# Memory's norm split around a merge, and low parts of weights moved to GpSimd

## The chip, the cores and the metric

The kernel runs on one core of one Trainium2 chip. The metric is device time in microseconds (us). The kernel before was run three times: 906.31, 908.57 and 908.62 us, median 908.57 us. The profile is of one more execution, which took 907.74 us.

## The reference, cut to what matters

The reference is one block of a network on 512 tokens of width 1024: a mixer of three attention branches, then attention to a memory of 256 rows, then a feed-forward part, each added to the stream, and a last norm. The change touches where the mixer's branches are merged and where memory's keys and values are made:

```python
merged = (g[:, :, 0] * (o_a @ w_up[0]) + g[:, :, 1] * (o_b @ w_up[1]) + g[:, :, 2] * (o_c @ w_up[2]))
h = h + merged @ w_out
kv = (_rmsnorm(mem, norm_mem_kv) @ w_mem_kv)      # 256 rows, 512 columns: keys and values
def _rmsnorm(x, g):
    return x * rsqrt(mean(x * x) + 1e-6) * g
```

Branch b is the one whose keys are selected by a top-k; its merge comes last.

## The kernel before, in words

All is float32. A weight or an activation goes to TensorE as two parts that the engine takes at a higher rate: a high part (`whi`, a rounding cast, L60) and a low part (`wlo`, the difference, L68). A product is three matmuls (`mm3`, L96 to L98): high by high, high by low, low by high. ScalarE (ACT) does the casts, VectorE (DVE) most of the differences, GpSimd (POOL) those of the weights that come through the ring `load_fill`. The other ring, `load_split`, has three buffers of 128x1024 each for the raw weights, the high parts and the low parts; a load of raw weights (SyncE's queue, SP) starts when the difference that read that buffer three loads before is done.

A list scheduler sets the order of the instructions on each engine when the kernel is built. Each engine then takes its list strictly in order, and an instruction waits on semaphores for what it needs.

The places that matter, in the order of the program:

- `fill_gate(1, f, S // 2)`: gates of branch b for the first 256 tokens; eight products into the PSUM tile `gf`, and TensorE's last work before memory's norm.
- Memory's norm. The 256 rows of `mem` are two chunks, `h[0]` and `h[1]`. For each, `norm_t` squares the chunk and sums it (ACT L129), turns the sum into a scale in eight VectorE instructions of 128x1 elements (`rms_scale`, L117 to L122, tile `rs`), multiplies (DVE L131, into `h[2]` or `h[3]`), transposes the result in eight 128x128 blocks (PE L135, tile `ps`), and splits it from PSUM into the two parts `mem_t`, which are the second halves of `mg_hi` and `mg_lo`.
- kv: 48 matmuls of 512 columns with four loads of `w_mem_kv` into two PSUM banks (tile `gm`), then copies, and transposes of the keys (L676 to L681).
- `merge_up(1, "b", ...)` for the first 256 tokens: for each of eight blocks f, six matmuls of 256 columns with `w_up` into a `gm` bank (two banks in turn), then on VectorE the sum with the gate (L388, reads PSUM and frees the bank) and an add (L401, both inputs in SBUF), then the split into `mg_hi` (ACT) and `mg_lo` (GpSimd).
- `w_out` for these tokens: 96 matmuls of 512 columns with eight loads of `w_out` (tile `wo`), then memory's attention for them (`memory_pair`). The other 256 tokens follow in the same way (`merge_rest`, `w_out`, `memory_pair`), then the feed-forward part.

Of the kernel before, what the change touches and what calls it, by code (L numbers as in the profile page):

```python
# [16 lines left out]
S = 512  # L17
D = 1024
# [8 lines left out]
def block_kernel(ctx: ExitStack, tc: tile.TileContext, A, out, dbg=None):  # L27
    nc = tc.nc
    w_in = A["w_in"][0]

    def pool(stack, name, side="left", **kw):
        return stack.enter_context(tc.tile_pool(name=name, bufs=1, side=side, reuse_waits="tile", **kw))
# [25 lines left out]
    def copy(eng, dst, src):  # L58
        if eng is nc.scalar:
            nc.scalar.copy(dst, src)  # L60
        else:
            eng.tensor_copy(dst, src)

    def split(dst_hi, dst_lo, src, hi_eng=None, lo_eng=None, scale=None):

        if scale is None:
            copy(hi_eng or nc.scalar, dst_hi, src)
            (lo_eng or nc.vector).tensor_sub(dst_lo, src, dst_hi.bitcast(F32))  # L68
        else:
            nc.scalar.activation(dst_hi, src, AF.Copy, scale=scale)  # L70
            nc.vector.scalar_tensor_tensor(dst_lo, src, scale, dst_hi.bitcast(F32), op0=ALU.mult, op1=ALU.subtract)

    def ring(pl, bufs, hi_eng=None, lo_eng=None):

        def load(shape, parts, lo_eng=lo_eng):
            n = shape[0] * shape[1]
            raw = pl.tile([P, WT], F32, name="raw", bufs=bufs[0])
            rv = raw[:, :n].rearrange("p (k n) -> p k n", n=shape[1])
            off = 0
            for src in parts:  # L80
                w = src.shape[-1]
                nc.sync.dma_start(rv[:, :, off:off + w], src)
                off += w
            hi = pl.tile([P, WT], F32R, name="whi", bufs=bufs[1])
            lo = pl.tile([P, WT], F32R, name="wlo", bufs=bufs[1])
            split(hi[:, :n], lo[:, :n], raw[:, :n], hi_eng, lo_eng)
            return [t[:, :n].rearrange("p (k n) -> p k n", n=shape[1]) for t in (hi, lo)]
        return load

    load_split = ring(stage, (3, 3))  # L90
# [14 lines left out]
    def col_view(w, c0, n):  # L105
        return w.rearrange("(k p) n -> p k n", p=P)[:, :, c0:c0 + n]

    def rms_scale(wk, ss, logs=False):

        v = wk.tile([P, 3], F32, name="rs", bufs=3)  # L110
        w, y, t = (v[:, i:i + 1] for i in range(3))
        if logs:
            nc.vector.tensor_scalar(w, ss, -0.5 / D, -0.5e-6, op0=ALU.mult, op1=ALU.add)
            nc.scalar.activation(y, ss, AF.Ln, bias=eps, scale=1.0 / D)
            nc.scalar.activation(y, y, AF.Exp, scale=-0.5)
        else:
            nc.vector.tensor_scalar(w, ss, 0.5 / D, 0.5e-6, op0=ALU.mult, op1=ALU.add)  # L117

            nc.vector.tensor_scalar(y.bitcast(I32), w.bitcast(I32), -0.5, 1597463007.0 - 2.0 ** 22 - 2.0 ** 31, op0=ALU.mult, op1=ALU.add)
        for _ in range(1 if logs else 3):  # L120
            nc.vector.scalar_tensor_tensor(t, y, w, y, op0=ALU.mult, op1=ALU.mult)
            nc.vector.scalar_tensor_tensor(y, t, 1.5 if logs else -1.5, y, op0=ALU.add, op1=ALU.mult)  # L122
        return y

    def norm_t(wk, ps, src, gain, dst, cols, logs=False, u=None):
        ss = wk.tile([P, 1], F32, name="ss", bufs=2)
        if u is None:
            u = wk.tile([P, D], F32, name="u", bufs=NT if logs else 2)
        nc.scalar.activation(u, src, AF.Square, accum_out=ss)  # L129
        y = rms_scale(wk, ss, logs)  # L130
        nc.vector.scalar_tensor_tensor(u, src, y, gain, op0=ALU.mult, op1=ALU.mult)  # L131
        for b in range(2):
            tp = ps.tile([P, 4, P], F32, name="ps")
            for k in range(4):
                nc.tensor.transpose(tp[:, k, :], u[:, (4 * b + k) * P:(4 * b + k + 1) * P], ident)  # L135
            split(dst[0][:, 4 * b:4 * b + 4, cols], dst[1][:, 4 * b:4 * b + 4, cols], tp)

    def load_gain(wk, name, bufs=1):
        g = A[name]
        g = g[0] if len(g.shape) == 2 else g  # L140
        t = wk.tile([P, D], F32, name="gain", bufs=bufs)
        nc.scalar.dma_start(t, g.partition_broadcast(P))
        return t
# [4 lines left out]
    def cc(c):  # L148
        return slice(c * P, (c + 1) * P)
# [7 lines left out]
    ps = p1.enter_context(tc.tile_pool(name="ps1", bufs=5, space=PSUM))  # L157
    gm_ps = gf_ps
# [29 lines left out]
    wk = pool(wk_st, "wk", side="right")  # L188
# [3 lines left out]
    gain = wk.tile([P, D], F32, name="gain")  # L192
# [7 lines left out]
    for c in range(NT):  # L200
        norm_t(wk, ps, xts[c], gain, uT, cc(c), logs=True)
# [178 lines left out]
    def load_up(j, fh, load):  # L380
        return load((2, 512), [A["w_up"][0, j].rearrange("(k p) n -> p k n", p=P)[:, :, fh * 512:(fh + 1) * 512]])

    def add_up(w, f, name, g, up, cols):

        fc = slice(f % 4 * P, f % 4 * P + P)
        for k in range(2):
            mm3(up, [t[:, k, fc] for t in w], [t[:, k, cols] for t in oT[name]], k == 0, k == 1)
        nc.vector.scalar_tensor_tensor(g, g, 1.0, up, op0=ALU.add, op1=ALU.mult)  # L388

    def merge_up(j, name, load, up_ps, n=S):  # L390
        for f in range(NK):
            if f % 4 == 0:
                w = load_up(j, f // 4, load)
            g, first = g_t[j, f][:, :n], g_t[0, f][:, :n]
            if j == 0 and f < early_g:
                with tc.issue_after(last_exp[0]):
                    nc.scalar.activation(g, g, AF.Tanh, scale=0.5)
            up = up_ps.tile([P, 512], F32, name=up_tag[up_ps is gf_ps])
            add_up(w, f, name, g, up[:, :n], slice(0, n))
            if j == 1:  # L400
                nc.vector.tensor_add(first, first, g)  # L401
                split(mg[0][:, f, :n], mg[1][:, f, :n], first, lo_eng=nc.gpsimd)
            elif j == 2:
                nc.gpsimd.tensor_add(first, first, g)
# [7 lines left out]
    ps = pm.enter_context(tc.tile_pool(name="ps2", bufs=3, space=PSUM))  # L412
    gm_ps = pm.enter_context(tc.tile_pool(name="gm_ps", bufs=2, space=PSUM))
# [237 lines left out]
    h = [hp_.tile([P, D], F32, name=f"h{c}") for c in range(NT)]  # L651
# [7 lines left out]
    mem_t = [t[:, :, half1] for t in mg]  # L659
    kv_st = ctx.enter_context(ExitStack())  # L660
    kvp = pool(kv_st, "kvp")
    for c in range(2):
        nc.scalar.dma_start(h[c], A["mem"][0, cc(c), :])
    gain = load_gain(kvp, "norm_mem_kv")
    for c in range(2):
        norm_t(kvp, ps, h[c], gain, mem_t, cc(c), u=h[2 + c])
    kv_acc = [gm_ps.tile([P, 512], F32, name="gm") for c in range(2)]
    for k2 in range(0, NK, 2):
        wh, wl = load_split((2, 512), [col_view(A["w_mem_kv"][0], 0, 512)[:, k2:k2 + 2, :]])
        for kk in range(2):  # L670
            for c in range(2):
                k = k2 + kk
                mm3(kv_acc[c], [t[:, k, cc(c)] for t in mem_t], (wh[:, kk, :], wl[:, kk, :]), k == 0, k == NK - 1)
# [7 lines left out]
        nc.vector.tensor_copy(vm[:, c, :], kvt[:, 256:512])  # L681
    kv_st.close()

    merge_up(1, "b", load_split, gm_ps, S // 2)
    first1 = [h[2 + f // 4][:, f % 4 * 256:f % 4 * 256 + 256] for f in range(NK)]
    for f in range(NK):
        nc.scalar.copy(first1[f], g_t[0, f][:, half1])
# [7 lines left out]
    ps = d_st.enter_context(tc.tile_pool(name="pd_ps", bufs=2, space=PSUM))  # L695
# [21 lines left out]
    def memory_pair(cs):  # L717
        pr = {}
        for c in cs:
            norm_t(md, ps, h[c], gain_q, uT, cc(c))  # L720
# [55 lines left out]
    for cp in range(2):  # L776
        cs = (2 * cp, 2 * cp + 1)
        if cp:
            merge_rest(0)
            merge_rest(1)  # L780
        for c in cs:
            nc.scalar.dma_start(h[c], A["x"][0, cc(c), :])
        ob = {(c, half): wo_ps.tile([P, 512], F32, name="wo") for c in cs for half in range(2)}
        for k in range(NK):
            w = load_split((1, D), [col_view(A["w_out"][0], 0, D)[:, k:k + 1, :]])
            for c in cs:
                for half in range(2):
                    n = slice(half * 512, half * 512 + 512)
                    mm3(ob[c, half], [t[:, k, cc(c)] for t in mg], [t[:, 0, n] for t in w], k == 0, k == NK - 1)
        for c in cs:  # L790
            for half in range(2):
                n = slice(half * 512, half * 512 + 512)
                nc.vector.tensor_add(h[c][:, n], ob[c, half], h[c][:, n])
        memory_pair(cs)
# [52 lines left out]
    y_out, gain = (utp.tile([P, NK, S], F32, name=n).rearrange("p a b -> p (a b)") for n in ("ut_hi", "ut_lo"))  # L847
    gain = gain[:, 0:D]
# [76 lines left out]
```

## Time and profile before

| | |
|---|---|
| median of 3 runs | 908.57 us (906.31 to 908.62) |
| profiled execution | 907.74 us, of which the span is 905.9 us |
| TensorE busy | 861.6 us, 95% of the span |
| VectorE, ScalarE, GpSimd busy | 508.0, 411.9, 139.6 us |
| mean granted TensorE clock | 0.989 of full |
| memory's norm to the end of the first `w_out` | about 377 to 428 us of the span |

The profile's timelines have one row for an instruction, or for several of one kind merged (xN): start, duration, engine, source line, operation, output and inputs; in brackets how long the engine sat idle before it and what ended that. An instruction's duration includes the time in which it was issued but held up. A table by stretches has, for each, from and to, its length, the busy time of PE, PEld, DVE, ACT and POOL (with the instructions), TensorE's granted clock as a part of full, the share of the DMA engines and GB/s. The chain of waits is followed back from the last instruction; its rows are start, length and what took it.

### The profile page before, as it was taken

Reading aid. Unit: us, or ns where it says so; the run is one execution under the profiler, and the core shown is the slowest. Engines: PE = TensorE matmul, PEld = TensorE weight load, DVE = VectorE, ACT = ScalarE, POOL = GpSimd, SP = SyncE. Lnnn points to the kernel's source line nnn. Section 1 sums busy time; section 2 is a strip of 40 time slices with the busy share of each in tenths; the row PEclk is TensorE's granted clock in tenths of the full one; section 3 lists DMA queues with packets and bytes.
Section 4 is the critical chain, followed back from the end, with each engine's and each line's share of the span. In section 5 each row is a group of like instructions: output and inputs, shape, how many; then the busy total and the mean of one; then the engine's idle time right before and its main releaser. Section 6 shows DMA issues by size and latency. Waiting matters only on the chain.

```text
span 905.9 us, 13081 instructions
## 1 busy us (share of the span) xinstructions
PE 861.6 (95%) x5012; PEld 734.7 (81%) x5012; DVE 508.0 (56%) x1155; ACT 411.9 (45%) x779; POOL 139.6 (15%) x116
## 2 busy tenths in 40 slices
PE   5999999899999999799989999999999999999995
PEld 5987899787677877787878879998888888888884
DVE  4466377689993058666677758653344443322226
ACT  6388545558872235454655555432322322211123
POOL 4021232201213472221232020000000000000002
PEclk9999999899999999999999999999999999999998
DMA  9240114410103331557455523553332333322312
GB/s 322 81 109 24 52 49 130 127 48 24 48 24 98 96 103 53 163 181 247 131 155 177 180 71 114 182 163 101 93 94 93 95 105 103 116 93 93 96 45 93
DMA packets 93710, 99.00 MB, mean 109 GB/s; under 512 B 4656, under 2 KB 81616, under 8 KB 93648
## 3 DMA queue, kind: packets, MB, share of 16 engines
q1 hardware_dynamic: 91568, 92.75, 33.7%
q10 hardware_dynamic: 2080, 5.42, 1.8%
q8 instruction: 39, 0.64, 0.3%
q14 instruction: 23, 0.19, 0.1%
HBM read 96.06 MB, written 2.10 MB: 108 GB/s over the span
## 4 chain that ended last, share of the span: by engine, by line
PE 82%; DVE 9%; ACT 3%; DMA 2%; issue 2%; POOL 0%; ACTq 0%; SPq 0%; DVEq 0%; POOLq 0%
PE wo L97 9%; PE wo L98 9%; PE wo L96 9%; PE gf L98 5%; PE gf L97 5%; PE gf L96 5%; PE ff L98 4%; PE ff L97 4%; PE ff L96 4%; PE gm L96 3%; PE gm L97 3%; PE gm L98 2%; PE av L103 2%; PE y L98 2%; PE y L97 2%; PE y L96 2%
## 5 line engine op out<-in xcount | busy, mean ns | idle before, releaser
L60 ACT CAST whi<-raw 128x1024 fp32r<-128x1024 f32 (+1 forms) x167 | 174.6, 1048 | 289.3 <-PE y L98 78.9
L68 DVE TENSOR_TENSOR wlo<-raw,whi 128x1024 fp32r<-128x1024 f32 (+1 forms) x131 | 164.4, 1257 | 207.4 <-ACT whi L60 207.2
L68 POOL TENSOR_TENSOR wlo<-raw,whi 128x1024 fp32r<-128x1024 f32 x36 | 87.9, 2446 | 329.7 <-ACT whi L60 279.3
L97 PE MATMUL wo<-ut_lo,whi 128*128 128x256 f32 (+1 forms) x320 | 106.1, 332 | 0.0
L98 PE MATMUL wo<-ut_hi,wlo 128*128 128x256 f32 (+1 forms) x320 | 105.2, 329 | 0.0
L96 PE MATMUL wo<-ut_hi,whi 128*128 128x256 f32 (+1 forms) x320 | 105.0, 328 | 0.0
L96 PE MATMUL gf<-ut_hi,whi 128*128 128x512 f32 (+1 forms) x192 | 69.9, 364 | 0.0
L97 PE MATMUL gf<-ut_lo,whi 128*128 128x512 f32 (+1 forms) x192 | 69.8, 364 | 0.0
L98 PE MATMUL gf<-ut_hi,wlo 128*128 128x512 f32 (+1 forms) x192 | 69.8, 363 | 0.0
L98 PE MATMUL ff<-ut_hi,wlo 128*128 128x512 f32 (+1 forms) x192 | 68.0, 354 | 0.0
L97 PE MATMUL ff<-ut_lo,whi 128*128 128x512 f32 (+1 forms) x192 | 68.0, 354 | 0.0
L96 PE MATMUL ff<-ut_hi,whi 128*128 128x512 f32 (+1 forms) x192 | 68.0, 354 | 0.0
L97 PEld LDWEIGHTS wo<-ut_lo,whi 128*128 128x128 f32 x320 | 61.6, 193 | 6.3 <-issue 1.0
L96 PEld LDWEIGHTS wo<-ut_hi,whi 128*128 128x128 f32 x320 | 61.5, 192 | 5.7 <-issue 0.7
L98 PEld LDWEIGHTS wo<-ut_hi,wlo 128*128 128x128 f32 x320 | 61.5, 192 | 5.5 <-issue 0.4
L874 POOL TENSOR_TENSOR ut_hi<-ut_hi,ut_lo 128x512 f32<-128x512 f32 x4 | 5.0, 1271 | 367.0 <-ACT ut_hi L873 367.0
L96 PE MATMUL gm<-whi,ut_hi 128*128 128x256 f32 (+1 forms) x160 | 47.7, 298 | 0.0
L97 PE MATMUL gm<-wlo,ut_hi 128*128 128x256 f32 (+1 forms) x160 | 47.2, 295 | 0.0
L98 PE MATMUL gm<-whi,ut_lo 128*128 128x256 f32 (+1 forms) x160 | 46.5, 291 | 0.0
L98 PEld LDWEIGHTS gf<-ut_hi,wlo 128*128 128x128 f32 x192 | 36.3, 189 | 6.7 <-issue 1.9
L96 PEld LDWEIGHTS gf<-ut_hi,whi 128*128 128x128 f32 x192 | 36.3, 189 | 6.0 <-issue 1.2
L97 PEld LDWEIGHTS gf<-ut_lo,whi 128*128 128x128 f32 x192 | 36.3, 189 | 5.3 <-issue 0.8
(329 smaller groups left out, 2032.0 us busy)
## 6 DMA issues: line engine op xcount, KB each, us to landing
raw<-in_w_ffn_in_dram SPq DMA_DIRECT2D x56, 512.0 KB, 3.6
raw<-in_w_in_dram SPq DMA_DIRECT2D x46, 512.0 KB, 3.9
raw<-in_w_ffn_out_dram SPq DMA_DIRECT2D x22, 512.0 KB, 3.6
raw<-in_w_out_dram SPq DMA_DIRECT2D x16, 512.0 KB, 3.6
raw<-in_w_up_dram SPq DMA_DIRECT2D x8, 512.0 KB, 4.3
xt<-in_x_dram SPq DMA_DIRECT2D x4, 512.0 KB, 9.1
raw<-in_w_mem_kv_dram SPq DMA_DIRECT2D x4, 512.0 KB, 3.7
raw<-in_w_mem_q_dram SPq DMA_DIRECT2D x4, 512.0 KB, 3.9
```

Of the source, the lines that this page charges most:

```text
L60: nc.scalar.copy(dst, src)
L68: (lo_eng or nc.vector).tensor_sub(dst_lo, src, dst_hi.bitcast(F32))
L96: nc.tensor.matmul(dst, lh, rh, start=first, stop=False, skip_group_check=True)
L97: nc.tensor.matmul(dst, lh, rl, start=False, stop=False, skip_group_check=True)
L98: return nc.tensor.matmul(dst, ll, rh, start=False, stop=last, skip_group_check=True).ins
L103: nc.tensor.matmul(dst[64 * x:64 * x + 64], lhs[x], rhs[x], start=first, stop=last, skip_group_check=True)
L874: nc.gpsimd.tensor_mul(yo[:, n], yo[:, n], gain[:, n])
```

## The change: what it does

`norm_t` is split into `norm_rows` (squares, scale, multiplication) and `turn` (transposes and the split into two parts). For memory, both chunks' `norm_rows` now stand first, then `merge_up(1, "b", ...)`, then both chunks' `turn`, then kv. So branch b's merge moves from behind kv to between the two parts of the norm. Three sets of weights' low parts change engine: the two of `w_up` in this merge go from VectorE to GpSimd, two of the four of `w_mem_kv`, and four of the eight of `w_out`, each of the two times that it is used. That is 12 instructions of 128x1024 elements more on GpSimd and 12 fewer on VectorE.

```diff
-    def norm_t(wk, ps, src, gain, dst, cols, logs=False, u=None):
+    def norm_rows(wk, src, gain, logs=False, u=None):
...
         nc.scalar.activation(u, src, AF.Square, accum_out=ss)
         y = rms_scale(wk, ss, logs)
         nc.vector.scalar_tensor_tensor(u, src, y, gain, op0=ALU.mult, op1=ALU.mult)
+        return u
+
+    def turn(ps, u, dst, cols):
         for b in range(2):
...
+    def norm_t(wk, ps, src, gain, dst, cols, logs=False):
+        turn(ps, norm_rows(wk, src, gain, logs), dst, cols)
...
     for c in range(2):
-        norm_t(kvp, ps, h[c], gain, mem_t, cc(c), u=h[2 + c])
+        norm_rows(kvp, h[c], gain, u=h[2 + c])
+    merge_up(1, "b", lambda *a: load_split(*a, lo_eng=nc.gpsimd), gm_ps, S // 2)
+    for c in range(2):
+        turn(ps, h[2 + c], mem_t, cc(c))
     kv_acc = [gm_ps.tile([P, 512], F32, name="gm") for c in range(2)]
     for k2 in range(0, NK, 2):
-        wh, wl = load_split((2, 512), [col_view(A["w_mem_kv"][0], 0, 512)[:, k2:k2 + 2, :]])
+        wh, wl = load_split((2, 512), [col_view(A["w_mem_kv"][0], 0, 512)[:, k2:k2 + 2, :]],
+                            (nc.vector, nc.gpsimd)[k2 // 2 % 2])
...
-    merge_up(1, "b", load_split, gm_ps, S // 2)
...
-            w = load_split((1, D), [col_view(A["w_out"][0], 0, D)[:, k:k + 1, :]])
+            w = load_split((1, D), [col_view(A["w_out"][0], 0, D)[:, k:k + 1, :]], (nc.vector, nc.gpsimd)[k % 2])
```

GpSimd's list at memory's norm, before. `wlo_4914` and `wlo_4944` are the low parts of `w_mem_q`, `mg_lo` those of the merged rows, `wlo_5071` is `w_mem_o`:

```order
L68 TENSOR_TENSOR wlo_4914<-raw_4911,whi_4913 128x1024
L68 TENSOR_TENSOR wlo_4944<-raw_4941,whi_4943 128x1024
L68 TENSOR_TENSOR mg_lo_4425<-g_1119,mg_hi_4424 128x256
L68 TENSOR_TENSOR mg_lo_4425<-g_1152,mg_hi_4424 128x256
L68 TENSOR_TENSOR mg_lo_4425<-g_1185,mg_hi_4424 128x256
```

The same place now. `wlo_4460` and `wlo_4510` are `w_up`, `wlo_4608` is the second load of `w_mem_kv`:

```order
L68 TENSOR_TENSOR wlo_4460<-raw_4457,whi_4459 128x1024
L68 TENSOR_TENSOR wlo_4510<-raw_4507,whi_4509 128x1024
L68 TENSOR_TENSOR wlo_4914<-raw_4911,whi_4913 128x1024
L68 TENSOR_TENSOR wlo_4944<-raw_4941,whi_4943 128x1024
L68 TENSOR_TENSOR mg_lo_4425<-g_1119,mg_hi_4424 128x256
L68 TENSOR_TENSOR mg_lo_4425<-g_1152,mg_hi_4424 128x256
L68 TENSOR_TENSOR mg_lo_4425<-g_1185,mg_hi_4424 128x256
L68 TENSOR_TENSOR wlo_4608<-raw_4605,whi_4607 128x1024
```

Two large instructions stand ahead of the two of `w_mem_q` now, and one between the third and the fourth `mg_lo`.

VectorE's list there, before, from the first chunk's multiplication (into `h2`) to the second's (into `h3`); `rs_4461` is the second chunk's scale, `wlo_4490` and `wlo_4508` are `w_mem_kv`:

```order
L131 SCALAR_TENSOR_TENSOR h2_4414<-h0_4412,rs_4435,gain_4431 128x1024
L122 SCALAR_TENSOR_TENSOR rs_4461<-rs_4461 128x1
L68 TENSOR_TENSOR wlo_4490<-raw_4487,whi_4489 128x1024
L121 SCALAR_TENSOR_TENSOR rs_4461<-rs_4461 128x1
L68 TENSOR_TENSOR wlo_4508<-raw_4505,whi_4507 128x1024
...
L131 SCALAR_TENSOR_TENSOR h3_4415<-h1_4413,rs_4461,gain_4431 128x1024
L68 TENSOR_TENSOR wlo_4526<-raw_4523,whi_4525 128x1024
L68 TENSOR_TENSOR mg_lo_4425<-ps_4445,mg_hi_4424 128x4x128
```

And now; between the two multiplications stand the five instructions of 128x1 (two are shown), and behind the second the merge's sums (L394) and adds (L407):

```order
L131 SCALAR_TENSOR_TENSOR h2_4414<-h0_4412,rs_4435,gain_4431 128x1024
L122 SCALAR_TENSOR_TENSOR rs_4447<-rs_4447 128x1
L121 SCALAR_TENSOR_TENSOR rs_4447<-rs_4447 128x1
...
L131 SCALAR_TENSOR_TENSOR h3_4415<-h1_4413,rs_4447,gain_4431 128x1024
L394 SCALAR_TENSOR_TENSOR g_4143<-g_4143,gm_4463 128x256
L68 TENSOR_TENSOR wlo_4590<-raw_4587,whi_4589 128x1024
L407 TENSOR_TENSOR g_1119<-g_1119,g_4143 128x256
L394 SCALAR_TENSOR_TENSOR g_4176<-g_4176,gm_4474 128x256
L394 SCALAR_TENSOR_TENSOR g_4209<-g_4209,gm_4485 128x256
```

The first sum, which frees the merge's first PSUM bank (`gm_4463`), stands behind the second chunk's multiplication.

TensorE's list behind the last gate product, before (`ps` are the transposes, `gm` is kv):

```order
L98 MATMUL gf_4375<-ut_hi_86,wlo_4379 128x256
L135 MATMUL ps_4445<-cst_67,h2_4414 128x128 x4
L135 MATMUL ps_4452<-cst_67,h2_4414 128x128 x4
L135 MATMUL ps_4471<-cst_67,h3_4415 128x128 x4
L96 MATMUL gm_4485<-whi_4489,mg_hi_4424 128x512
L97 MATMUL gm_4485<-wlo_4490,mg_hi_4424 128x512
```

And now, from the end of the merge's third block (`gm_4485` is that block here) on; ahead of it stand the last gate product and the two first blocks, `gm_4463` and `gm_4474`, of six matmuls each:

```order
L98 MATMUL gm_4474<-o_hi_3923,wlo_4460 128x256
L96 MATMUL gm_4485<-o_hi_3923,whi_4459 128x256
L97 MATMUL gm_4485<-o_lo_3924,whi_4459 128x256
L98 MATMUL gm_4485<-o_hi_3923,wlo_4460 128x256
...
L138 MATMUL ps_4557<-cst_67,h2_4414 128x128 x4
L138 MATMUL ps_4564<-cst_67,h2_4414 128x128 x4
L138 MATMUL ps_4571<-cst_67,h3_4415 128x128
L96 MATMUL gm_4496<-o_hi_3923,whi_4459 128x256
```

The first chunk's transposes moved from directly behind the gates to behind the third block, which needs the first block's bank again.

## Rows read from the trace of the kernel before

**Rows 1.** The page's first part: busy time, share and instructions of each engine.
```profile
PE 861.6 (95%) x5012; PEld 734.7 (81%) x5012; DVE 508.0 (56%) x1155; ACT 411.9 (45%) x779; POOL 139.6 (15%) x116
```

**Rows 2.** TensorE's timeline, memory's norm to `w_out` (in brackets idle before, releaser).
```profile
377.24 1.04 PE L135 MATMUL ps<-cst,h 128*128 128x128 f32 x8
383.44 1.09 PE L135 MATMUL ps<-cst,h 128*128 128x128 f32 x4 [5.16 <-DVE h L131]
...
388.82 0.40 PE L96 MATMUL gm<-whi,mg_hi 128*128 128x512 f32 x1
...
396.76 0.39 PE L98 MATMUL gm<-whi,mg_lo 128*128 128x512 f32 x1
...
409.11 0.50 PE L97 MATMUL wo<-wlo,mg_hi 128*128 128x512 f32 x1 [0.64 <-DVE wlo L68]
...
417.32 0.50 PE L97 MATMUL wo<-wlo,mg_hi 128*128 128x512 f32 x1 [0.42 <-DVE wlo L68]
```

**Rows 3.** The chain of waits, 376 to 429: start, length, what.
```profile
376.99 2.27 DVE rs L122
...
397.59 0.12 PE gm L96
...
428.06 0.24 PE wo L98
```

**Rows 4.** VectorE's timeline, 373 to 384.
```profile
373.24 1.28 DVE L131 SCALAR_TENSOR_TENSOR h<-h,rs,gain 128x1024 f32<-128x1024 f32 x1
...
374.50 1.22 DVE L68 TENSOR_TENSOR wlo<-raw,whi 128x1024 fp32r<-128x1024 f32 x1
...
376.90 2.34 DVE L122 SCALAR_TENSOR_TENSOR rs<-rs 128x1 f32<-128x1 f32 x1
379.28 2.26 DVE L121 SCALAR_TENSOR_TENSOR rs<-rs 128x1 f32<-128x1 f32 x1
381.58 0.16 DVE L122 SCALAR_TENSOR_TENSOR rs<-rs 128x1 f32<-128x1 f32 x1
382.01 1.28 DVE L131 SCALAR_TENSOR_TENSOR h<-h,rs,gain 128x1024 f32<-128x1024 f32 x1 [0.27 <-DVE rs L122]
```

**Rows 5.** GpSimd's timeline, 368 to 384.
```profile
376.13 5.39 POOL L68 TENSOR_TENSOR wlo<-raw,whi 128x1024 fp32r<-128x1024 f32 x2 [14.23 <-ACT whi L60]
```

**Rows 6.** ScalarE's timeline, 372 to 398.
```profile
372.85 1.99 ACT L60 CAST whi<-raw 128x1024 fp32r<-128x1024 f32 x2
...
375.01 1.99 ACT L60 CAST whi<-raw 128x1024 fp32r<-128x1024 f32 x2
...
396.51 1.26 ACT L676 COPY h<-gm 128x512 f32<-128x512 f32 x2 [0.98 <-PE gm L98]
```

**Rows 7.** VectorE's and GpSimd's timelines, 470 to 474.
```profile
470.83 2.31 DVE L122 SCALAR_TENSOR_TENSOR rs<-rs 128x1 f32<-128x1 f32 x1
...
470.74 2.40 POOL L68 TENSOR_TENSOR wlo<-raw,whi 128x1024 fp32r<-128x1024 f32 x1 [0.90 <-POOL wlo L68]
```

**Rows 8.** VectorE's timeline, 384 to 409.
```profile
384.35 1.88 DVE L68 TENSOR_TENSOR mg_lo<-ps,mg_hi 128x512 fp32r<-128x512 f32 x3
...
398.66 0.41 DVE L388 SCALAR_TENSOR_TENSOR g<-g,gm 128x256 f32<-128x256 f32 x1
399.11 0.43 DVE L401 TENSOR_TENSOR g<-g 128x256 f32<-128x256 f32 x1
...
405.97 0.74 DVE L388 SCALAR_TENSOR_TENSOR g<-g,gm 128x256 f32<-128x256 f32 x2
406.63 1.28 DVE L401 TENSOR_TENSOR g<-g 128x256 f32<-128x256 f32 x2
```

**Rows 9.** Three stretches in which TensorE's granted clock was below full.
```profile
384.00:388.00 4.00, 4.00 (x16) 2.98 (x15) 2.44 (x5) 2.64 (x8) 0.00 (x0) 0.64 0.56 168
...
470.00:476.00 6.00, 3.74 (x31) 3.54 (x30) 5.68 (x12) 3.19 (x6) 2.40 (x1) 0.97 0.58 168
476.00:482.00 6.00, 6.00 (x41) 6.00 (x40) 4.75 (x10) 2.42 (x5) 0.00 (x0) 0.75 0.35 100
```

## The prediction

> **What bounds the kernel now.** First the page's busy times: TensorE is busy for 95% of the span [rows 1], so a change gains by closing one of its few holes, or loses by opening one. Then TensorE's own timeline around memory's norm. Its first row is the first chunk's transposes at 377.24, directly behind the gates; then nothing until 383.44, a hole of 5.16 us that VectorE's multiplication ends (L131, into `h`), and two small waits of 0.64 and 0.42 us in `w_out` [rows 2]. Next the chain of waits: inside the hole it names a VectorE instruction of 128x1 elements, 2.27 us long [rows 3]. VectorE's own timeline shows the reason. The same kind of instruction takes 0.16 us at 381.58, but 2.34 and 2.26 us at 376.90 and 379.28 [rows 4], and those two lie just where GpSimd runs the two low parts of `w_mem_q`, 376.13 to 381.52 [rows 5]. The second L122 ends at 379.24 and the L121 behind it starts at 379.28 and is held again to 381.54: between two GpSimd instructions one small instruction gets in, not two. At 470.83 it happens once more, 2.31 us beside a GpSimd instruction of 2.40 [rows 7]. Last the stretches: behind the hole the granted clock of 384 to 388 was 0.64 [rows 9], that is a part of it at the lower level of 1.2 GHz.
>
> The Trainium skill, "SBUF — State Buffer", section "SBUF: two separate sides", says that VectorE and GpSimd share one pair of ports under an exclusive lock, which whoever starts first holds for the whole instruction while the other is blocked, if VectorE has two SBUF inputs. The trace agrees: 2.34 us for an instruction of 0.16 [rows 4]. It speaks against this change, which puts more GpSimd work beside that chain.
>
> **The change, step by step.** The sum is made on the profiled execution, 907.74 us, which is 0.83 below the median of 908.57. I follow TensorE from 377.24, the end of the gates, to the end of the first `w_out`, which before is 428.06 + 0.24 = 428.3 [rows 3]. Up to 373 the lists of TensorE, VectorE and ScalarE are the same, only SyncE loads `w_up` where it loaded `w_mem_kv`, so these rows are kept.
>
> *The norm's arithmetic, +2.0.* Removed between the two multiplications: two low parts on VectorE, 1.22 us each [rows 4]. Added ahead of `w_mem_q` on GpSimd: the two low parts of `w_up`. Their casts take the place of the two at 372.85, those of `w_mem_q` stay at 375.01 and are done at 377.0 [rows 6], so GpSimd has four large instructions ready one behind the other. One takes (381.52 - 376.99) / 2 = 2.27 us, counted from 376.99, where the chain has the first small instruction begin to be held [rows 3, 5]. The first waits for the first chunk's multiplication, 373.24 + 1.28 = 374.5, and the four last until 374.5 + 4 x 2.27 = 383.6. VectorE has five small instructions to do before the second multiplication; one gets in behind each GpSimd instruction, so the fourth comes at 383.6. The fifth and the multiplication follow as before: 0.43 from the one's start to the other's, and 1.28 [rows 4]. End: 385.3, before it was 383.3.
>
> *TensorE's hole, 7.0 instead of 5.2.* TensorE now does two blocks of the merge first, 12 matmuls at 0.12 [rows 3], 1.4 us, until 378.7. The third block needs the first block's bank, which VectorE's sum frees, and that sum is queued behind the second multiplication: 385.3 + 0.41 [rows 8] = 385.7. The transposes of the first chunk, which were done in time before, are queued behind the third block on TensorE, and ScalarE's copies and casts behind those transposes.
>
> *The merge, now in VectorE's hands.* Before kv can run, VectorE has eight sums at 0.33 from start to start, eight adds at about 0.36 (0.43 with its tail), one low part at 1.2 and three of memory's four low parts at 0.63 [rows 4, 8]. Up to the eighth sum, which frees kv's second bank: 2.6 + 2.5 (seven adds) + 1.2 + 1.3 (two parts) = 7.6 us if nothing waits. Before, eight sums, eight adds and one low part (6.7 us by the same prices) took from 398.66 to 407.9 [rows 8], 9.25 us, since adds wait for GpSimd's `mg_lo` and sums for TensorE: a factor of 1.37. I take it over: 10.4, so 395.7. New here is a GpSimd low part of 2.27 between the third and the fourth `mg_lo`, in which an add can be held: 0 to 2.27, no row tells which; I take half, 1.1, so 396.8, and one more of memory's parts, so 397.7. By then kv has done 3 of its 48 matmuls. On TensorE this phase holds only 36 matmuls of 0.12 and the transposes, some 6 us, so nothing of it shows as TensorE's work.
>
> *kv and `w_out`.* A matmul of 512 columns takes (396.76 - 388.82) / 35 = 0.227 us (36 matmuls from the one row to the other) [rows 2]. kv: 397.7 + 45 x 0.227 = 407.9. Then the second chunk's copy out of PSUM, 0.63 [rows 6], and two transposes, 0.25, which before lay beside the merge's matmuls and have no cover now: 408.8. `w_out`: 96 x 0.227 = 21.8, without the waits of 0.64 and 0.42 [rows 2], because its weights' parts are ready during kv: 430.6. Against 428.3 that is +2.3.
>
> *The clock.* Behind the longer hole TensorE runs at 1.2 GHz for some time as before; this now falls into the phase that VectorE sets, so I count nothing. A second hole, TensorE's wait for the merge's end (about 2 us), can lower the clock in kv. The nearest row: 2.3 us idle before 476, then 0.75 over 6 us [rows 9], which costs 6 x 0.25 = 1.5. So 0 to 1.5; I take 0.3, since in this phase TensorE is only partly idle.
>
> *`w_out`'s low parts on GpSimd.* Eight times one cast (1.0) and 2.40 instead of 1.22 [rows 4, 6, 7]. The buffer comes free two loads of TensorE work, 2 x 12 x 0.227 = 5.4, before the part is needed, so 2 us of slack hide it; VectorE's 10 us saved lie off the path, for TensorE is what `w_out` waits for. If the cover fails, it costs about 0.6 for each of the eight. Beside `merge_rest` a low part can hold an add, but `mg_lo` has time until the fifth load of `w_out`.
>
> Sum: +2.0 reaches TensorE as +1.8 of idle, and the merge's phase, exposed, takes the rest; 2.3 + 0.3 = **+2.6 us**. 907.74 + 2.6 = 910.3, and on the runs' median 908.57 + 2.6 = **911.2 us**.
>
> **Rivals.**
> - *GpSimd doesn't hold VectorE up* (the other side: faster). Place: the five small instructions behind 374.5. Then the second multiplication ends at about 376.5, TensorE never waits, merge and transposes end near 385.7 (VectorE's 9.2 us from 376.5), kv at 396.6, `w_out` at 419.3: -9.0, or about -6 if `w_out`'s loads, first issued at 391 before, come late. 900 to 903 us. It decides from the point where two small instructions fit between two GpSimd ones. Against it stand three held instructions [rows 4, 7]. The same rule of the skill, "SBUF — State Buffer", excludes it as well.
> - *The merge flows* (no change). The factor is 1 and no add is held: 385.3 + 7.6 + 0.6 = 393.5 in place of 397.7, so -1.9 + 0.3: 907.0. For it: GpSimd's `mg_lo` are spread wider than before. Against: ScalarE takes the casts in order and stands behind the transposes.
> - *The merge and the clock both go badly* (slower by more). The whole 2.27 is paid (+1.2), kv starts at 1.2 GHz (+1.2), and a late ScalarE cast of `w_mem_kv` costs another 1: +6.0, 914.6.
> - *GpSimd's `w_out` parts come late*: 4 to 8 x 0.6 = 2.4 to 4.8 more, 913.6 to 916.0. Against it the 2 us of slack.
> - *The hold at 470.83 falls away*, because all around it shifts: TensorE's 2.3 us there and part of the clock's 1.5 come back, -2 to -3.5 on the sum. For it, only that the timing moves; against, that the cast which starts that GpSimd instruction moves along.
>
> **How the numbers follow.** Within 0.3%, 2.7 us, is about what measurements of this kernel can't tell from no change. The forecast, +1 to +4.5: 0.55, with its middle at 2.6, so half of it, 0.28, is slower by over 2.7. The merge flows: 0.16, same. Both go badly 0.12 and late `w_out` parts 0.05, slower. No hold: 0.06, faster. The hold at 470 falls away: 0.06, half faster, half same, since it sets off the sum. Slower 0.28 + 0.17 = 0.45, faster 0.09, rounded up to 0.13 for what isn't thought of, same 0.42. The range reaches from the merge that flows, 906.6, to the bad case, 914.6; what lies outside is no hold, late parts and half of the last rival. The forecast's own range is 909.6 to 913.1.
>
> **What will show it.** In the profile after: four GpSimd low parts from about 374.5 to 383.6; four VectorE instructions of 128x1 of over 2 us; the second multiplication's end at 385 (at 377 the first rival has won); a TensorE hole of about 7 us ended by VectorE's L394; kv running freely from about 397.7 (at 393.5 the merge flowed); `w_out` without waits; its end near 430.9. I am wrong in the mechanism if the small instructions are short or if the hole is under 5 us, and wrong in the size if the merge's phase, from the second multiplication to kv, is far from 12 us.

## The result, and the profile after

The changed kernel took 915.88 us (median of 4 runs, 914.43 to 916.43), the kernel before beside it 908.01 us: a ratio of 1.0088 with a 95% interval of 1.0074 to 1.0101, so 7.9 us slower. The forecast was 911.2 us with a range up to 914.6. The profiled execution took 916.43 us, its span was 914.6 us, against 907.74 and 905.9 before, 8.7 us more.

Page, first part, after (compare [rows 1]): VectorE is busy 6.2 us less, although 12 differences of 1.22 us left it, since the time in which an instruction is held counts as busy; GpSimd is busy 25.9 us more. TensorE is busy 1.8 us longer with the same 5012 matmuls, at a mean granted clock of 0.984 where it was 0.989.

```profile
PE 863.4 (94%) x5012; PEld 736.6 (81%) x5012; DVE 501.8 (55%) x1143; ACT 412.7 (45%) x779; POOL 165.5 (18%) x128
```

VectorE's timeline after, at memory's norm (compare [rows 4]): four small instructions of over 2 us in place of two, then the second multiplication.

```profile
375.23 2.38 DVE L122 SCALAR_TENSOR_TENSOR rs<-rs 128x1 f32<-128x1 f32 x1
377.65 2.31 DVE L121 SCALAR_TENSOR_TENSOR rs<-rs 128x1 f32<-128x1 f32 x1
379.99 2.26 DVE L122 SCALAR_TENSOR_TENSOR rs<-rs 128x1 f32<-128x1 f32 x1
382.29 2.26 DVE L121 SCALAR_TENSOR_TENSOR rs<-rs 128x1 f32<-128x1 f32 x1
384.59 0.16 DVE L122 SCALAR_TENSOR_TENSOR rs<-rs 128x1 f32<-128x1 f32 x1
384.78 1.28 DVE L131 SCALAR_TENSOR_TENSOR h<-h,rs,gain 128x1024 f32<-128x1024 f32 x1
```

GpSimd's timeline after (compare [rows 5]): four low parts in one piece, and later the first low part of `w_out`.

```profile
374.77 9.76 POOL L68 TENSOR_TENSOR wlo<-raw,whi 128x1024 fp32r<-128x1024 f32 x4 [12.34 <-ACT whi L60]
...
409.41 2.35 POOL L68 TENSOR_TENSOR wlo<-raw,whi 128x1024 fp32r<-128x1024 f32 x1 [5.52 <-ACT whi L60]
```

TensorE's timeline after, from the hole to the end of `w_out` (compare [rows 2]): the hole of 7.10 us, kv's first matmul, kv's last, then the transposes of kv's keys (L689), `w_out`'s first matmul and its last.

```profile
386.45 0.58 PE L96 MATMUL gm<-o_hi,whi 128*128 128x256 f32 x1 [7.10 <-DVE g L394]
...
396.56 0.47 PE L96 MATMUL gm<-whi,mg_hi 128*128 128x512 f32 x1 [1.60 <-ACT mg_hi L60]
...
407.51 0.39 PE L98 MATMUL gm<-whi,mg_lo 128*128 128x512 f32 x1
409.87 0.93 PE L689 MATMUL ps<-cst,h 128*128 128x128 f32 x4 [1.97 <-ACT h L686]
412.82 0.79 PE L96 MATMUL wo<-whi,mg_hi 128*128 128x512 f32 x1 [2.03 <-DVE km L690]
...
437.07 0.39 PE L98 MATMUL wo<-whi,mg_lo 128*128 128x512 f32 x1
```

Up to kv's end the steps are within 0.9 us of the forecast. Then TensorE waits 1.97 us for ScalarE and 2.03 us for VectorE. ScalarE's timeline shows the first wait's cause: the copies of kv out of PSUM (L686) come behind a cast that waited 4.69 us for a load of `w_out`.

```profile
408.28 1.05 ACT L60 CAST whi<-raw 128x1024 fp32r<-128x1024 f32 x1 [4.69 <-DMA raw<-in_w_out_dram]
409.24 1.06 ACT L686 COPY h<-gm 128x512 f32<-128x512 f32 x2
```

That load, `w_out`'s second, was issued at 401.0 and took 7.2 us to land. Beside it ScalarE's queue had two loads of 512 KB each, the gains of the next norms. The DMA issues of 400 to 402 (KB each, median us from issue to landing):

```profile
gain<-in_norm_mem_q_dram ACTq DMA_DIRECT2D x1, 512.0 KB, 4.3
gain<-in_norm_ffn_dram ACTq DMA_DIRECT2D x1, 512.0 KB, 5.2
raw<-in_w_out_dram SPq DMA_DIRECT2D x1, 512.0 KB, 7.2
```

VectorE's timeline shows the second wait's cause. The copy into `vm` takes 2.06 us and ends with GpSimd's low part of 409.41; the next copy of the same size takes 0.28. Behind the long one stands the copy (L690) that frees the PSUM tile of `w_out`'s first bank.

```profile
409.85 2.06 DVE L691 COPY vm<-h 128x256 f32<-128x256 f32 x1 [4.87 <-ACT h L686]
411.83 0.41 DVE L690 COPY km<-ps 128x256 f32<-128x256 f32 x1
412.16 0.28 DVE L691 COPY vm<-h 128x256 f32<-128x256 f32 x1
```

The Trainium skill, "SBUF — State Buffer", section "Who interferes with whom", says that copies can enter a mode in which they too need the pair of ports shared with GpSimd, and that the second comer is blocked wholly. The trace agrees: 2.06 us instead of 0.28.

The stretches after (columns as in [rows 9]): the granted clock is 0.94, 0.50 and 0.71 from 408 to 420, so that `w_out` begins at 1.2 GHz.

```profile
404.00:408.00 4.00, 3.90 (x18) 2.89 (x16) 0.97 (x1) 0.00 (x0) 0.00 (x0) 1.00 1.01 399
408.00:412.00 4.00, 0.87 (x4) 0.40 (x4) 2.15 (x2) 2.02 (x3) 2.35 (x1) 0.94 0.19 74
412.00:416.00 4.00, 3.18 (x8) 2.50 (x9) 1.99 (x4) 1.05 (x1) 0.00 (x0) 0.50 0.79 280
416.00:420.00 4.00, 4.00 (x14) 3.21 (x13) 0.00 (x0) 1.05 (x1) 0.52 (x1) 0.71 0.62 245
```

`w_out` ends at 437.07 + 0.24 = 437.3, before at 428.3 [rows 3]: 9.0 us later, nearly the 8.7 us of the spans. Of these 9.0, 0.5 were there ahead of the changed part: a wait of TensorE for VectorE that stands in both traces ends at 331.71 before and at 332.22 after.

### The profile page after: what moved, and what is told of

It is laid out like the page before. It is cut to its first block, busy times and chain, and to the rows that moved or that the text cites. A ratio compares the mean times of both kernels' runs of the same rounds, so it can differ in the third digit from the quotient of the medians.

```text
span 914.6 us, 13083 instructions
## 1 busy us (share of the span) xinstructions
PE 863.4 (94%) x5012; PEld 736.6 (81%) x5012; DVE 501.8 (55%) x1143; ACT 412.7 (45%) x779; POOL 165.5 (18%) x128
## 4 chain that ended last, share of the span: by engine, by line
PE 49%; DVE 4%; ACT 1%; issue 1%; DVEq 0%; ACTq 0%
PE wo L96 9%; PE wo L97 9%; PE wo L98 9%; PE ff L97 4%; PE ff L98 4%; PE ff L96 4%; PE y L96 2%; PE y L97 2%; PE y L98 2%; PE ps L138 1%; PE mm L96 1%; PE mm L98 1%; PE mm L97 1%; DVE rs L121 1%; DVE rs L122 1%
## 5 line engine op out<-in xcount | busy, mean ns | idle before, releaser
L68 DVE TENSOR_TENSOR wlo<-raw,whi 128x1024 fp32r<-128x1024 f32 (+2 forms) x119 | 149.3, 1255 | 216.7 <-ACT whi L60 216.6
L68 POOL TENSOR_TENSOR wlo<-raw,whi 128x1024 fp32r<-128x1024 f32 x48 | 116.6, 2434 | 337.7 <-ACT whi L60 298.8
```

## The experiments

The theory read from the trace: GpSimd's four parts lengthen the norm (as forecast), and most of the loss arises between kv and `w_out`, where a late load holds ScalarE's queue and a GpSimd part holds VectorE, with a slow clock behind. Ratios are to runs of the kernel before in the same comparison. Line numbers are each kernel's own, so the same line can differ by a few.

One thing varies between the traces that no edit touches: when the load of memory's second chunk lands. ScalarE squares that chunk at 369.6 in one trace and at 372.6 in another, VectorE's first multiplication follows it, and TensorE's hole grows or shrinks with it. After the change it was late:

```profile
372.32 1.06 ACT L129 ACTIVATE h<-h 128x1024 f32<-128x1024 f32 x1 [1.44 <-DMA h<-in_mem_dram]
```

So a hole's length in one trace says little by itself. What doesn't move with the load is the time from the end of the first multiplication to the end of the second: 8.77 us before, 10.75 after.

**One part of the change alone: `w_out`'s low parts.** The kernel before, with

```diff
-            w = load_split((1, D), [col_view(A["w_out"][0], 0, D)[:, k:k + 1, :]])
+            w = load_split((1, D), [col_view(A["w_out"][0], 0, D)[:, k:k + 1, :]], (nc.vector, nc.gpsimd)[k % 2])
```

> The kernel before, with one edit of the change alone: four of the eight low parts of w_out on GpSimd, each of the two times. Theory (the change's loss lies in four GpSimd parts that lengthen memory's norm, and in two waits between kv and w_out that the new order makes, the late copy out of PSUM and VectorE's copy vm held by GpSimd's first w_out part, with the half clock behind them): here the merge stands between kv and w_out as before, so nothing is held there; w_out's waits of 1.1 us in all change by under 1 us; 908 (907 to 910), VectorE's busy time down by some 8 to 10 us and nothing gained by it. Rival A (GpSimd's slower w_out parts themselves cost, about 0.6 us for each of eight): w_out waits for POOL wlo several times, 911 to 913.

909.25 us against 907.61, ratio 1.0026 (1.0013 to 1.0040). That is inside the theory's range and below rival A's, but the waits changed by more than the 1 us expected. TensorE's waits (total, times, longest) for `w_out`'s parts are 2.5 us, where they were 1.1:

```profile
PE wo L97 <- POOL wlo L68: 2.5, 2, 1.9
```

So the parts were not wholly hidden. The wait of 1.9 us is not the engine's alone: the chain of waits has ahead of it a load of `w_out` that took 7.20 us, from 409.19, then the cast, then the part of 2.37 us on GpSimd, which takes 1.22 on VectorE. Most of the loss is elsewhere.

**The move alone.** The change with

```diff
-    merge_up(1, "b", lambda *a: load_split(*a, lo_eng=nc.gpsimd), gm_ps, S // 2)
+    merge_up(1, "b", load_split, gm_ps, S // 2)
```

and `w_mem_kv` and `w_out` without the choice of engine.

> The move alone: the norm in two parts with the merge between, all low parts of w_up, w_mem_kv and w_out on VectorE as before. Theory: only the two w_mem_q parts hold the norm's small instructions, so the hole before the merge's third block is about 5 to 6 us in place of 7.1; the copy vm between kv and w_out takes 0.3 us and not 2.1, w_out starts 1.5 to 2 us nearer to kv's end, and the clock behind it stays higher: 910 to 912.5 against 915.9 of the whole change, still not below 908. Rival B (the move itself is the cost, since VectorE alone sets the merge and kv): 914 to 918. Rival C (GpSimd is all of the cost): 908 or below.

911.69 us, ratio 1.0055 (1.0039 to 1.0072). The time is the one expected, the way to it in part not. The two longest waits of TensorE behind 374:

```profile
PE gm L96 <- DVE g L394: 3.9, 1, 3.9
PE ps L688 <- ACT h L685: 3.0, 1, 3.0
```

The hole shrank to 3.9 us, more than expected: the norm from the first multiplication's end to the second's took 8.85 us, 1.9 less than with the whole change, and memory's load landed 1.5 us sooner in this trace. kv's last matmul was at 403.05, 4.5 us sooner than with the whole change, but the wait for ScalarE grew to 3.0, because the copies stand behind casts that wait for loads of `w_out` there too: what kv gained was partly lost at its end. Rival C falls: without any of the moved GpSimd parts it is still slower. Rival B falls too: the move without them costs 0.55%, the whole change 0.88%.

**The change with `w_out`'s low parts back on VectorE.** The edit of the first experiment, undone in the change.

> The whole change, but w_out's low parts on VectorE as before (w_up and two of w_mem_kv stay on GpSimd). Theory: hole of 7 us before the merge's third block unchanged, kv ends at about 407.9 as in the whole change; the copy vm takes 0.3 us in place of 2.06, so w_out starts at about 411 instead of 412.8, and a part of the half clock behind it goes: 912 to 914.5. The ScalarE copy out of PSUM is still late behind the cast that waits for w_out's load. Rival D (the held vm copy costs nothing, the late load of w_out is the whole wait and the clock falls anyway): 915.5 to 917.

912.31 us, ratio 1.0058 (1.0043 to 1.0073), in the theory's range. The hold of `vm` is gone:

```profile
409.68 0.29 DVE L691 COPY vm<-h 128x256 f32<-128x256 f32 x1
```

The wait for L690 is 0.9 instead of 2.0 us; that for ScalarE stays at 1.9. Not as expected, the hole is shorter and kv ends at 407.1, 0.8 us sooner than in the whole change:

```profile
385.12 0.58 PE L96 MATMUL gm<-o_hi,whi 128*128 128x256 f32 x1 [5.84 <-DVE g L394]
```

That isn't the edit's doing, since memory's load landed sooner here; the norm itself took 10.77 us, as with the whole change. Without these 0.8 us the time would still be below rival D's 915.5, so rival D falls, but not all that this run gained belongs to `vm`.

**The gains' loads later.** The change, with

```diff
-        nc.scalar.copy(kvt, kv_acc[c])
+        kvc = nc.scalar.copy(kvt, kv_acc[c]).ins
...
-    gain_q = load_gain(md, "norm_mem_q", 2)
-    gain_f = load_gain(md, "norm_ffn", 2)
+    with tc.issue_after(kvc):
+        gain_q = load_gain(md, "norm_mem_q", 2)
+        gain_f = load_gain(md, "norm_ffn", 2)
```

where `issue_after` puts what it holds behind that copy on ScalarE's queue.

> The whole change, with the two loads of the norms' gains (512 KB each) issued by ScalarE behind kv's copies instead of during kv. Theory (the second w_out load lands late, ScalarE's cast that waits for it stands ahead of kv's copies out of PSUM, and the two gain loads share the DMA engines with it): that cast comes 1.5 to 2.5 us earlier (about 406 instead of 408.3), kv's copies start at kv's end, 407.9, GpSimd's low part of w_out lies earlier beside nothing that matters, w_out starts at 409.5 to 411 instead of 412.8, and the clock behind it recovers in part: 911 to 914 against 915.9. Rival F (the load is late only because it is issued late, the gains take nothing from it): 915 to 917.

912.11 us, ratio 1.0052 (1.0037 to 1.0067): the theory. The same load now lands 5.0 us after its issue at 399.97 instead of 7.2:

```profile
raw<-in_w_out_dram SPq DMA_DIRECT2D x1, 512.0 KB, 5.0
```

ScalarE's cast comes at 405.06 and the copies need not wait for it; TensorE's wait for them is 0.24. The hold of `vm` stays (1.85 us):

```profile
407.54 0.44 PE L689 MATMUL ps<-cst,h 128*128 128x128 f32 x2 [0.24 <-ACT h L686]
409.61 0.50 PE L96 MATMUL wo<-whi,mg_hi 128*128 128x512 f32 x1 [1.63 <-DVE km L690]
```

So the gains' loads made that load 2.2 us later; in the traces of the run above and of the next, which have them beside it, it takes 7.0. Rival F falls.

**kv's copies ahead of the cast.** The change with `kvc` as above, the gains' loads as in the change, and

```diff
+            with tc.issue_after(kvc) if cp == 0 and k else ExitStack():
                 w = load_split((1, D), [col_view(A["w_out"][0], 0, D)[:, k:k + 1, :]], (nc.vector, nc.gpsimd)[k % 2])
```

> The whole change, with one order fixed by hand: ScalarE does kv's two copies out of PSUM before the cast of the second w_out load; all loads as in the change. Theory (queue order makes the wait): the copies start at kv's end (407.9 to 408.2), the transposes' wait of 1.97 falls to about 0.7, VectorE's copy vm takes 0.3 instead of 2.06, since GpSimd's part now comes behind it, w_out starts at 409.3 to 410; then up to 2 us may be lost where w_out's second step waits for its low part: 911 to 914. Rival G (the late load only moves the wait into w_out, nothing is gained): 915 to 917, w_out waiting 3 us or more for POOL wlo.

910.66 us, ratio 1.0034 (1.0020 to 1.0047), a little better than expected. No load is sooner (`w_out`'s second was issued at 401.85 and took 7.0 us); the order on ScalarE is what was set. Of TensorE's waits of 1.97 and 2.03 us, 0.24 and 0.52 are left, the second because VectorE's copy into `vm` now comes ahead of GpSimd's part and takes 0.29 us:

```profile
409.26 0.44 PE L689 MATMUL ps<-cst,h 128*128 128x128 f32 x2 [0.24 <-ACT h L686]
410.22 0.50 PE L96 MATMUL wo<-whi,mg_hi 128*128 128x512 f32 x1 [0.52 <-DVE km L690]
```

and the clock is full in the stretch that had 0.50:

```profile
412.00:416.00 4.00, 4.00 (x19) 3.32 (x18) 2.58 (x1) 1.20 (x2) 3.28 (x2) 1.00 0.68 238
```

`w_out` takes 410.22 to 432.1, 21.9 us, as forecast. Rival G falls: nothing of the wait came back inside `w_out`. What is left of the loss, 910.66 - 907.58 = 3.1 us, is near the forecast's 2.6.

**The kernel before, with `w_mem_q`'s low parts on VectorE.**

```diff
-            w = load_fill((4, 256), [col_view(A["w_mem_q"][0], 0, 256)[:, 4 * kh:4 * kh + 4, :]])
+            w = load_fill((4, 256), [col_view(A["w_mem_q"][0], 0, 256)[:, 4 * kh:4 * kh + 4, :]], nc.vector)
```

> The kernel before, with the low parts of w_mem_q on VectorE in place of GpSimd (both times that it is used), so no large GpSimd instruction lies beside memory's norm. Theory (shared pair of ports, one instruction excludes the other): the two instructions of 128x1 that took 2.34 and 2.26 us take 0.16; VectorE has two low parts of 1.2 us more in that chain instead, so TensorE's hole of 5.2 us becomes 2 to 3.5 us, and the 2.3 us wait at 470 becomes 0 to 1.3; with some clock back: 903 to 906. Rival E (the small instructions are long for another reason, such as a wait that the profile does not name): they stay at over 2 us, and the time is 908 or above, since VectorE has more to do.

898.84 us, ratio 0.9911 (0.9896 to 0.9925): 8.8 us faster than before, more than expected; only a variant below, which can't be told from it, has a lower median. VectorE's timeline (compare [rows 4]) has the low parts at 1.2 us and the small instructions between them short again:

```profile
373.72 0.15 DVE L122 SCALAR_TENSOR_TENSOR rs<-rs 128x1 f32<-128x1 f32 x1
373.79 1.22 DVE L68 TENSOR_TENSOR wlo<-raw,whi 128x1024 fp32r<-128x1024 f32 x1
374.93 0.21 DVE L121 SCALAR_TENSOR_TENSOR rs<-rs 128x1 f32<-128x1 f32 x1
...
379.87 0.15 DVE L122 SCALAR_TENSOR_TENSOR rs<-rs 128x1 f32<-128x1 f32 x1
```

The second multiplication still ends only at 381.07 + 1.28 = 382.35, some 0.9 us sooner than before, and 0.7 of that the trace has already at the first one: between the two stand five low parts of weights now, where two stood before, and two of memory's. Yet TensorE waits only 0.90 and 0.17 us, and the clock from 384 to 388, 0.64 before [rows 9], is full. What goes with it is a second effect of the edit: the scheduler now puts kv's first chunk between the two chunks' transposes, so TensorE has work until the second multiplication is done.

```profile
378.50 0.50 PE L96 MATMUL gm<-whi,mg_hi 128*128 128x512 f32 x1 [0.90 <-ACT mg_hi L60]
378.84 0.40 PE L97 MATMUL gm<-wlo,mg_hi 128*128 128x512 f32 x1
379.41 0.50 PE L98 MATMUL gm<-whi,mg_lo 128*128 128x512 f32 x1 [0.17 <-DVE mg_lo L68]
```

**The same at the first place only**: `(nc.gpsimd, nc.vector)[cs[0] == 0]` in place of `nc.vector`.

> The kernel before, with the low parts of w_mem_q on VectorE only the first time that they are used (beside memory's norm); the second time, beside the norm at 470, they stay on GpSimd. Theory (each place has its own hold): the hole at 377 goes from 5.2 us to about 1, with 1.4 us of clock behind it, and the wait of 2.3 us with its clock (0.62 over 4 us, 1.5 us) stays: 902 to 903.5, so 5 to 5.5 of the 8.8 us that both places gave together. Rival J (the gain is the clock's, or one place gives all): 898 to 900, or above 905.

901.65 us, ratio 0.9936 (0.9920 to 0.9952), a little under the theory's range. So memory's norm gives 5.7 us and the norm at 470 the other 3; the 2.3 us wait there is still in this kernel's trace, behind L131 in place of L117. Engine and order changed together in both, so two more runs take them apart.

**`w_mem_q` on VectorE, TensorE's list at the norm as before.** Every kv matmul is put behind the fourth transpose of the second chunk (`first_tr`):

```diff
-                mm3(kv_acc[c], [t[:, k, cc(c)] for t in mem_t], (wh[:, kk, :], wl[:, kk, :]), k == 0, k == NK - 1)
+                with tc.issue_after(first_tr[0]):
+                    mm3(kv_acc[c], [t[:, k, cc(c)] for t in mem_t], (wh[:, kk, :], wl[:, kk, :]), k == 0, k == NK - 1)
```

> The kernel before with w_mem_q's low parts on VectorE (898.8), but TensorE's list at memory's norm as it was before: both chunks' transposes ahead of kv. Taking the parts off GpSimd had also made the scheduler put kv's first chunk between the two chunks' transposes. VectorE's list is unchanged by this edit. If the gain at memory's norm is that order on TensorE: the hole is back at 4.5 to 5.2 us (the second multiplication ends at 382.4, only 1 us sooner than before), with half clock behind it, 903 to 905. If the shorter chain on VectorE alone is the gain: 900 or below.

904.49 us, ratio 0.9967 (0.9958 to 0.9977). The hole is back, and 3.1 us of gain are left, as much as the place at 470 gives:

```profile
383.61 1.94 PE L137 MATMUL ps<-cst,h 128*128 128x128 f32 x8 [4.72 <-DVE h L133]
```

**The new order with GpSimd as before.** Only the order at memory's norm is changed: `norm_rows(h[0])`, `turn`, `norm_rows(h[1])` with its multiplication behind the first chunk's `mg_lo`, kv's first two loads for the first chunk, the second `turn`, the rest of kv.

> The kernel before with all engines as they were (w_mem_q's low parts on GpSimd), but the order changed by hand: kv's first two loads for the first chunk stand between the two chunks' transposes on TensorE, and the first chunk's low parts (mg_lo) ahead of the second multiplication on VectorE. If the order alone is the gain: 901 to 903. If VectorE must be free for it too (the held instructions of over 2 us stand ahead of a w_mem_kv part and both mg_lo, so TensorE's third kv matmul waits until about 383.4): the hole is 4 to 5 us and the time 905 to 908.

907.30 us, ratio 0.9995 (0.9983 to 1.0007): no change. TensorE gets its kv matmul sooner and then waits for the low part that stands behind the held instructions on VectorE:

```profile
380.11 0.50 PE L96 MATMUL gm<-whi,mg_hi 128*128 128x512 f32 x1 [0.90 <-ACT mg_hi L60]
384.06 0.50 PE L98 MATMUL gm<-whi,mg_lo 128*128 128x512 f32 x1 [3.22 <-DVE mg_lo L68]
```

So neither half gains at memory's norm: an order that gives TensorE work needs a VectorE that is free to prepare it.

**`w_mem_o`'s low parts on VectorE as well.** The `load_fill` of `w_mem_o` gets `nc.vector` too.

> The kernel before, with the low parts of w_mem_q on VectorE, and those of w_mem_o too. Theory: w_mem_o's parts on GpSimd (436 to 442 us) hold no instruction that TensorE waits for, so this is no gain: 898 to 900 against 898.8. Rival K (every large GpSimd instruction costs): 896 to 897.

898.13 us, ratio 0.9901 (0.9884 to 0.9917), whose interval overlaps that of the run without it. No gain is shown, and rival K's 896 to 897 is not reached.

**The move without GpSimd beside the norm.** The move alone, with `w_mem_q`'s low parts on VectorE.

> The move with no weights' low part on GpSimd beside the norm at all: w_up, w_mem_kv, w_out and w_mem_q all on VectorE. Theory: no small instruction is held, the second multiplication ends near 380.5, the hole before the third block is about 2 us, the 2.3 us wait at 470 goes too; the wait between kv and w_out (about 4 us, cast ahead of copies) stays, with half clock behind it: 902 to 906, so slower than the kernel before with w_mem_q alone on VectorE (898.8). Rival H (the move pays once nothing is held): 898 or below.

904.45 us, ratio 0.9965 (0.9952 to 0.9978). The time is in the theory's range, but the wait is in another place: not at kv's end (`w_out` starts 1.6 us behind it) but inside kv, for the low part of its second load, which VectorE does behind all of the merge's adds:

```profile
389.19 0.47 PE L96 MATMUL gm<-whi,mg_hi 128*128 128x512 f32 x1 [1.28 <-ACT mg_hi L60]
392.10 0.80 PE L97 MATMUL gm<-wlo,mg_hi 128*128 128x512 f32 x1 [2.44 <-DVE wlo L68]
```

Rival H falls. Even with nothing held, the move is 5.6 us slower than the order of before with the same engines (904.45 against 898.84).

**That, with both repairs at kv's end.**

> The run above (move, all low parts on VectorE) with both repairs: the gain loads behind kv's copies and the cast of the second w_out load behind them too. Theory: the wait between kv and w_out falls from some 4 us to about 1, the clock there stays full: 3 to 5 us less than the run above, 897 to 901, about as fast as the kernel before with w_mem_q on VectorE. Rival I (the cost lies in the merge phase that VectorE sets, not at kv's end): within 1.5 us of the run above.

903.42 us, ratio 0.9959 (0.9945 to 0.9973): the theory is wrong here, rival I holds. There was little left to repair at kv's end. By its trace the loss lies in the merge phase that VectorE sets: a wait of 1.2 us for ScalarE and one of 2.4 us for the low part in kv, and a granted clock of 0.50 from 392 to 396 behind them. Which of VectorE's instructions in that phase could be moved was not tried.

## Why the prediction was wrong

Its steps, one by one, all on the span's clock:

| step | forecast | after |
|---|---|---|
| four GpSimd parts | 374.5 to 383.6 | 374.8 to 384.5 |
| second multiplication ends | 385.3 | 386.1 |
| TensorE's hole | 7.0 us | 7.1 us |
| kv ends | 407.9 | 407.9 |
| `w_out` starts | 408.8 | 412.8 |
| `w_out` takes | 21.8 us | 24.5 us |
| `w_out` ends | 430.9 with the clock's 0.3 | 437.3 |

- **The holds and the hole: right**, and so is the order of the merge. The small instructions take over 2 us each, one behind each GpSimd part. The norm's +2.0 was measured almost exactly: 10.75 us from multiplication to multiplication, 8.77 before. The 0.8 us by which the second one ended later than forecast lie ahead of the change: 0.5 that the trace has at 332, the rest memory's late load.
- **The merge phase: right in its end, in part by luck.** An add was held, 1.95 us instead of 0.42, so 1.5 where I took 1.1. The eighth sum ended at 398.0, where the forecast had 396.8, but kv's first bank had started at 396.56, so that six matmuls were done by then and not three. From the second multiplication's end to kv's end it took 21.8 us where the sum had 22.6, which set off the 0.8 us of the late start.
- **The step that failed is the one behind kv: "the second chunk's copy out of PSUM, 0.63 [rows 6], and two transposes, 0.25", with the result 408.8.** It priced the instructions and put the waits in the queues in which they stand at nothing. On ScalarE a cast that needs a load stands ahead of the copies, and on VectorE GpSimd's first `w_out` part excludes the copy behind them: 412.8 - 408.8 = 4.0 us. The same step says of `w_out` that "its weights' parts are ready during kv"; its second load was issued at 401.0 and landed 7.2 us later, beside the two gain loads. Changing only the order on ScalarE takes the ratio from 1.0088 to 1.0034, about 4.9 us; moving only the gains' loads takes it to 1.0052, about 3.3 us.
- **The clock: too small.** I allowed 0.3, with 1.5 as the end, for a wait in the merge phase. The wait fell between kv and `w_out` instead, and `w_out` took 24.5 - 21.8 = 2.7 us longer, 2.4 beyond what was allowed. With the wait, 4.0 + 2.4 = 6.4 us, which is all of the miss on this clock (437.3 - 430.9). When the order on ScalarE is put right, both go, and 3.1 us of loss are left where 2.6 were forecast.
- **`w_out`'s parts on GpSimd, "so 2 us of slack hide it": not wholly.** They cost a ratio of 1.0026 alone. In the change TensorE waits for none of them inside `w_out`, but the first of them held `vm`.
- **The rivals.** "The merge and the clock both go badly" gave 914.6, near the result, by other places: kv started on time and at full clock. "GpSimd's `w_out` parts come late" gave 913.6 to 916.0, which holds the result, but by chance: `w_out` had no such wait. "The merge flows" would have had kv run freely from 393.5, and it began at 396.56; the range's lower end, 906.6, leaves out the 0.3 of the clock that this rival's own sum, 907.0, has in it. "GpSimd doesn't hold VectorE up" is excluded by the rows. The hold at 470 stayed (2.3 us, L138 behind L117).

## What to carry to other kernels

When a stage is moved, follow each engine's queue at the new seam, and ask of each instruction ahead of the one on the path what it waits for: here a cast for a load that TensorE didn't need yet, ahead of copies that it did need, cost 4.9 us, more than the whole forecast of 2.6. Before giving GpSimd more, look for short VectorE instructions beside its long ones: a chain of 0.2 us steps became one of 2.3 us steps. Taking GpSimd away from both norms, with the order that the scheduler then chose, was worth 8.8 us; at memory's norm neither the free VectorE nor the new order gained anything alone. Of an edit that changes a scheduler's order as well, run both halves apart before naming the cause.

## What the runs showed of the hardware

- Two loads of 512 KB on one queue made a load of 512 KB on another land about 2 us later (7.0 to 7.2 us in three traces, 5.0 without them), with the DMA engines' share at 1.01 from 404 to 408 after the change.
- Of two VectorE copies of the same 128x256 from SBUF to SBUF, the one beside a GpSimd difference took 2.06 us, the other 0.28. Sums with one input in PSUM (L394) were not held beside such a difference, the add behind them with both in SBUF (L407) was. VectorE's timeline after:

```profile
392.61 0.75 DVE L394 SCALAR_TENSOR_TENSOR g<-g,gm 128x256 f32<-128x256 f32 x2
393.27 1.95 DVE L407 TENSOR_TENSOR g<-g 128x256 f32<-128x256 f32 x1
```

and GpSimd's there:

```profile
392.31 2.62 POOL L68 TENSOR_TENSOR wlo<-raw,whi 128x1024 fp32r<-128x1024 f32 x1
```

- After the gap of 4.9 us between kv and `w_out`, with 0.93 us of transposes in it, the granted clock was 0.50 from 412 to 416; after one of 2.7 us with the same transposes (the gains' loads later) it was 0.80 from 408 to 412 and 0.78 from 412 to 416, and after one of 1.6 us (kv's copies first) it stayed at 1.00.
